# A list schedule that knows the port shared by VectorE and GpSimd, in a one-core decoder layer

## The chip, the core and the metric

The kernel runs on one core of a Trainium2 chip. A core has five engines that run side by side: TensorE (PE, matmuls), VectorE (DVE), ScalarE (ACT), GpSimd (POOL) and SyncE (SP, which only issues transfers here). The metric is the device time of one execution, in microseconds (us).

## What is computed

The reference is one layer of a decoder, 1024 tokens by 1024 features, float32. Cut to what matters:

```python
shift1, scale1, gate1, shift2, scale2, gate2 = silu(c) @ w_ada + b_ada
h = rms_norm(x, norm1) * (1 + scale1) + shift1
q, kc_raw, vc_raw, ks, vs, kw, vw, g, cgate, bgate, u = split(h @ w_in)
# 8 heads, 2 key/value heads; three branches per row of queries
o_c = softmax(q @ compress(kc_raw) + bias) @ compress(vc_raw)
o_s = softmax(q @ ks + bias, causal) @ vs         # blocks of 64; all 16 blocks are selected
o_w = softmax(q @ kw + bias, window 512) @ vw
attn = g[0] * o_c + g[1] * o_s + g[2] * o_w
conv = bgate * conv1d(cgate * u)                  # depthwise, 3 taps
x = x + gate1 * (concat(attn, conv) @ w_out)
h2 = rms_norm(x, norm2) * (1 + scale2) + shift2
out = x + gate2 * (square(relu(h2 @ w_ff1)) @ w_ff2)
```

## The kernel before

Everything is kept feature by feature: a tile has 128 features as partitions and 512 tokens (one half of the sequence) as columns. Every float32 matmul is made of three: an operand is split into a rounded part `hi` (a CAST, by `copy`) and a rest `lo` (a subtraction, by `sub`), and `mm3` adds hi x hi, hi x lo and lo x hi in one PSUM bank. So each 128x512 tile that TensorE reads costs one cast and one subtraction first, weights too.

The stages are, in the order of the program: the opening (adaLN's first part, the norm, and the first three column tiles of the projection); keys, values, queries and the compressed keys; attention of the first half of the tokens, with the convolution's matmuls beside it; attention of the second half, beside which the output projection of the first half and 30 tiles of the MLP's hidden layer are worked out; output projection and second norm of the second half; and the MLP. In the opening, `ada` loads a piece of `w_ada` and VectorE makes a product with a sum over 1024 columns (FA<-FA 128x1024, line 339), from which come one column of `mod` and one of `a`; then each tile k of x is multiplied with the norm (x*y, FA<-FA,FA), scaled by ScalarE, and split. In attention, the sum of a score and its bias is made on VectorE from PSUM (line 358), `nm`, `den` and `cf` are small tiles of three columns per row of queries, the row is scaled by `cf` (line 351 on GpSimd), transposed in blocks of 32 on VectorE (line 365), shuffled by sixteen transfers (FA<-FA, by SP) and split for the product with the values.

No order is written by hand. `Plan` takes down every instruction with a cost in ns and the engines that may run it (`alts`); `issue` makes eight list schedules (`_forward`, each with priorities from a schedule made from the end by `_backward`), keeps the one with the shortest span, and issues each engine's queue in that order. Many casts, subtractions, products and scalings may go to one of two engines (`EW` is VectorE or GpSimd); the schedule gives such an instruction to whichever engine is free first. On the chip each queue then runs strictly in order, and engines wait for each other by semaphores where data demands it. `issue` is called twice: once for everything up to the second norm, and once for the MLP. Memory is a few big tiles cut by hand: FA (FA1, FA2) is float32, RA holds the split operands, `sc`, `fa`, `po`, `stb` and (in the MLP) `pd` are PSUM banks.

Lines that the text speaks of: 293 is every matmul, 311 and 317 are ScalarE's activations and copies, 319 and 321 casts on VectorE and GpSimd, 328 and 330 two-input additions, subtractions and products on VectorE and GpSimd, 339 VectorE's scalar_tensor_tensor, 347 and 351 tensor_scalar on VectorE and GpSimd, 377 every transfer.

Of the kernel before, what the change touches and what calls it, by code (L numbers as in the profile page):

```python
# [37 lines left out]
# ---------------------------------------------------------------- the order of the instructions  # L38
class Op:
    __slots__ = ("alts", "idx", "preds", "succs", "nbytes", "past", "end", "group")  # L40
# [6 lines left out]
class Plan:  # L47
    """Takes down instructions in program order, then issues them in the order of a list schedule.

    An instruction may be taken by any of the engines listed for it.  What depends on what follows  # L50
    from the memory that the instructions read and write.  The first schedule goes by the longest way
    to the end; the next ones by where a schedule made from the end puts the instructions.
    """

    PASSES = 8
    # from the end of an instruction to the start of one that needs it, by their engines
# [5 lines left out]
    def __init__(self, tc):  # L62
        self.tc, self.nc = tc, tc.nc
        self.eng = {"PE": self.nc.tensor, "ACT": self.nc.scalar, "DVE": self.nc.vector,
                    "POOL": self.nc.gpsimd, "SP": self.nc.sync}
        self.ops, self.mem, self.scratch = [], {}, set()
        self.group, self.ahead = "", {}  # how much earlier than its turn a group of instructions goes
        self.free = {e: 0.0 for e in self.eng}  # when the engines are through with what was issued before

    # -- recording  # L70
    @staticmethod
    def _mask(ap):
        """{group of partitions: (first column, last column + 1, columns as bits)}"""
        dims = [tuple(d) for d in ap.ap]
        off = ap.offset
        if ap.space == PSUM:  # one accumulation group at a time in a bank
            return {0: (0, 1, 1)}
# [38 lines left out]
    def op(self, alts, outs, ins, nbytes=0):  # L116
        o = Op(alts, len(self.ops), nbytes)
        o.group = self.group
        for aps, wr in ((ins, False), (outs, True)):
            for ap in aps:  # L120
# [7 lines left out]
                for po, pm, pw in log:  # L128
                    if (wr or pw) and po is not o and self._hit(m, pm):
                        if po.end is None:  # L130
                            o.preds.add(po)
                        else:  # issued before
# [7 lines left out]
    # -- the schedule  # L140
# [3 lines left out]
    def _longest(self):  # L144
        """The longest way from each instruction to the end."""
# [7 lines left out]
    def _forward(self, prio):  # L153
        """[(start, instruction, choice, end)]: whenever an engine is free, the first by priority of those that are ready."""
# [5 lines left out]
        done, order, hw, dma, last, cold = bytearray(len(ops)), [], 0.0, 0.0, self.free["PE"], 0.0  # L160
# [15 lines left out]
        while len(order) < len(ops):  # L176
# [14 lines left out]
            _, idx, i = heapq.heappop(heaps[e])  # L191
            o, cost = ops[idx], ops[idx].alts[i][1]
            done[idx] = 1
            if not o.nbytes:
                if e == "PE":  # at half its rate after a rest
# [5 lines left out]
            else:  # L201
# [7 lines left out]
                if e == "SP":  # what is moved next is left open until its turn is near  # L209
# [10 lines left out]
    def _backward(self, order):  # L220
        """From the end, the last first: how long before the end each instruction starts."""
# [54 lines left out]
    # -- the instructions  # L276
# [11 lines left out]
    def mm(self, out, a, b, start, stop):  # L288
        n, m = self._n(out), self._n(a)
        c = max(0.4167 * n + 2, 107.0)  # L290
# [22 lines left out]
    def copy(self, out, a, engs=("ACT",)):  # L313
# [8 lines left out]
        self.op(alts, [out], [a])  # L322

    def tt(self, out, a, b, op, engs=("DVE",)):
# [6 lines left out]
        self.op(alts, [out], [a, b])  # L331
# [4 lines left out]
    def stt(self, out, a, s, b, op0, op1, accum=None):  # L336
# [3 lines left out]
                [out] + ([accum] if accum is not None else []), [a, b] + ([s] if ptr else []))  # L340

    def ts(self, out, a, s1, s2, op0, op1=None, engs=("DVE",)):
        n, ps, alts = self._n(out), self._ps(a, out), []
        ptr = sum(hasattr(s, "tensor") for s in (s1, s2))
        for e in engs:
# [6 lines left out]
            else:  # a product with one number for each partition  # L352
                alts.append((e, 0.833 * n + 93 + 93 * ptr, lambda: self.nc.scalar.activation(out, a, AF.Copy, scale=s1)))
        self.op(alts, [out], [a] + [s for s in (s1, s2) if hasattr(s, "tensor")])
# [25 lines left out]
class Rot:  # L380
    """A fixed set of tiles, taken in turn."""
# [9 lines left out]
class Region:  # L391
    """A stretch of columns of a tile, handed out from its left end."""
# [20 lines left out]
# columns (of 4 bytes) of the two tiles that everything of the first part lies in  # L413
# [961 lines left out]
```

## Time and profile before

| | |
|---|---|
| time, median of three runs | 1439.66 us (1437.44 to 1443.62) |
| span of the profiled execution, first to last instruction | 1439.1 us |
| instructions | 17186 |
| TensorE busy, mean granted clock | 1293.1 us, 0.955 |
| VectorE busy | 827.2 us |
| ScalarE busy | 608.0 us |
| GpSimd busy | 584.7 us |
| moved by DMA | 220.66 MB, mean 153 GB/s |

The profiled execution's own time is not given apart from its span, which is 0.6 us below the median. An instruction's time in the profile runs from its start on the engine to its end; what it waits for by semaphore comes before the start and is listed as idle time. A wait that the engine takes after the start is part of the duration.

### The profile page before, as it was taken

The page shows a single profiled execution, that of the slowest core. Times are in us where ns is not written, and L with a number is a line of the kernel's source. Part 1 is how long each engine was busy: PE and PEld are TensorE (multiplying, and loading weights), DVE is VectorE, ACT ScalarE, POOL GpSimd, SP SyncE. Part 2 cuts the span into 40 slices and gives each one's busy share as a digit, 9 for nine tenths or more (in the row PEclk, how much of TensorE's full clock was granted, in tenths as well). Part 3 has the DMA queues.
Part 4 walks back from the last instruction along what each step waited for, and adds up shares of the span by engine and source line. Part 5 has one row for each costly group of instructions (what it writes and reads, how often), then busy time and mean ns, then how long its engine had stood idle before and what let it go on. Part 6 is the DMA issues. An engine that isn't in the chain of part 4 may idle for free.

```text
span 1439.1 us, 17186 instructions
## 1 busy us (share of the span) xinstructions
PE 1293.1 (90%) x5608; PEld 1032.0 (72%) x5608; DVE 827.2 (57%) x1697; ACT 608.0 (42%) x1191; POOL 584.7 (41%) x581
## 2 busy tenths in 40 slices
PE   6689899899889888888797897989999999999998
PEld 3468688677667656666675684868888878888886
DVE  5987878789757675668784747541441252133212
ACT  5566647666536465646664434420130022103100
POOL 4733636587637574536574514111221221222120
PEclk8999999999999999989999897989999999999999
DMA  8567976887676864777769613441430232123131
GB/s 290 159 165 211 248 228 214 205 212 199 191 207 194 244 154 151 195 187 190 215 154 251 218 59 123 138 135 30 128 107 30 77 118 70 59 73 103 30 117 59
DMA packets 110029, 220.66 MB, mean 153 GB/s; under 512 B 14841, under 2 KB 40994, under 8 KB 109428
## 3 DMA queue, kind: packets, MB, share of 16 engines
q1 hardware_dynamic: 106196, 204.76, 49.5%
q0 software_dynamic: 3744, 14.81, 3.6%
q8 instruction: 44, 0.72, 0.2%
q14 instruction: 45, 0.37, 0.1%
HBM read 151.77 MB, written 36.80 MB: 131 GB/s over the span
## 4 chain that ended last, share of the span: by engine, by line
PE 49%; DVE 19%; DMA 13%; SPq 7%; issue 5%; POOL 4%; ACT 3%; DVEq 0%; POOLq 0%; ACTq 0%
PE pd L293 35%; SPq L377 7%; PE sc L293 7%; DMA FA<-FA 5%; PE fa L293 5%; DVE RA L328 5%; DVE FA L339 4%; DVE FA L365 3%; DVE FA L328 2%; POOL RA L330 2%; DMA FA<-in_w_ff 2%; DVE FA L358 2%; ACT FA L311 1%; DMA FA<-in_xT 1%; DMA FA<-in_w_ada 1%
## 5 line engine op out<-in xcount | busy, mean ns | idle before, releaser
L330 POOL TENSOR_TENSOR RA<-FA,RA 128x512 fp32r<-128x512 f32 (+4 forms) x193 | 336.5, 1752 | 521.1 <-ACT RA L317 228.2
L317 ACT CAST RA<-FA 128x512 fp32r<-128x512 f32 (+4 forms) x327 | 233.7, 736 | 587.0 <-PE pd L293 279.9
L293 PE MATMUL fa<-RA 128*128 128x512 f32 (+1 forms) x1384 | 411.6, 406 | 23.0 <-ACT FA L311 11.0
L293 PE MATMUL sc<-RA 128*128 128x512 f32 (+6 forms) x1328 | 338.1, 373 | 40.1 <-DVE mx L358 11.7
L293 PE MATMUL pd<-hid,RA 128*128 128x512 f32 x1344 | 339.5, 392 | 0.0
L293 PEld LDWEIGHTS fa<-RA 128*128 128x128 f32 (+1 forms) x1384 | 265.4, 196 | 86.7 <-ACT FA L311 14.0
L328 DVE TENSOR_TENSOR RA<-FA,RA 128x512 fp32r<-128x512 f32 (+4 forms) x214 | 215.5, 1018 | 193.2 <-PE pd L293 90.0
L293 PEld LDWEIGHTS sc<-RA 128*128 128x128 f32 x1328 | 239.5, 196 | 97.4 <-DVE mx L358 16.7
L293 PEld LDWEIGHTS pd<-hid,RA 128*128 128x128 f32 x1344 | 255.0, 190 | 53.4
L293 PE MATMUL pd<-RA 128*128 128x512 f32 x1008 | 267.9, 397 | 12.8 <-DVE RA L319 6.0
L293 PEld LDWEIGHTS pd<-RA 128*128 128x128 f32 x1008 | 191.0, 191 | 59.0 <-DVE RA L328 8.4
L339 DVE SCALAR_TENSOR_TENSOR FA<-pd,mod,FA 128x512 f32<-128x512 f32 x64 | 45.3, 746 | 219.2 <-PE pd L293 219.2
L311 ACT ACTIVATE FA<-FA,nm 128x640 f32<-128x640 f32 (+7 forms) x192 | 114.4, 597 | 42.9 <-DVE nm L347 22.0
L365 DVE STREAM_TRANSPOSE FA<-FA 128x64 f32<-128x64 f32 (+7 forms) x224 | 99.5, 482 | 41.2 <-DMA FA<-FA 23.0
L311 ACT ACTIVATE FA<-FA 128x512 f32<-128x512 f32 (+2 forms) x147 | 87.7, 616 | 25.2 <-DVE FA L339 14.6
L293 PE MATMUL stb<-RA 128*128 128x512 f32 (+1 forms) x192 | 68.5, 401 | 32.3 <-ACT RA L317 18.7
L351 POOL TENSOR_SCALAR FA<-FA,cf 128x64 f32<-128x64 f32 (+8 forms) x121 | 83.4, 701 | 21.7 <-DVE cf L328 18.3
L358 DVE CUSTOM_DVE_ANT_0 FA<-sc,FA 128x64 f32<-128x64 f32 (+5 forms) x192 | 79.9, 449 | 10.5 <-PE sc L293 10.1
L293 PE MATMUL po<-RA 128*128 128x512 f32 (+4 forms) x164 | 51.3, 380 | 21.7 <-ACT RA L317 15.9
L293 PEld LDWEIGHTS stb<-RA 128*128 128x128 f32 x192 | 36.9, 199 | 46.6 <-ACT RA L317 20.0
L321 POOL TENSOR_SCALAR RA<-FA 128x512 fp32r<-128x512 f32 x42 | 31.4, 748 | 88.2 <-DMA FA<-in_w_ff 42.8
L319 DVE CAST hid<-FA 128x512 fp32r<-128x512 f32 x56 | 42.0, 752 | 36.3 <-PE pd L293 18.8
(129 smaller groups left out, 897.6 us busy)
## 6 DMA issues: line engine op xcount, KB each, us to landing
FA<-in_w_ff SPq DMA_DIRECT2D x64, 512.0 KB, 3.6
FA<-FA SPq DMA_DIRECT2D x128, 176.0 KB, 4.0
FA<-in_w_ada SPq DMA_DIRECT2D x64, 256.0 KB, 3.9
FA<-in_w_ff SPq DMA_DIRECT2D x60, 256.0 KB, 3.8
FA<-FA SPq DMA_DIRECT2D x64, 208.0 KB, 5.2
FA<-in_w_cols SPq DMA_DIRECT2D x34, 256.0 KB, 2.9
FA<-in_xT SPq DMA_DIRECT2D x32, 256.0 KB, 4.8
FA<-in_w_ada SPq DMA_DIRECT2D x16, 512.0 KB, 3.6
```

The costliest lines, as they stand in the source:

```text
L293: self.op([("PE", c, lambda: self.nc.tensor.matmul(out, a, b, start=start, stop=stop))], [out], [a, b])
L311: self.op([("ACT", c, lambda: self.nc.scalar.activation(out, a, func, **kw))], outs, ins)
L317: alts.append((e, 0.833 * n + (53 if ps else 93), lambda: self.nc.scalar.copy(out, a)))
L319: alts.append((e, (1.04 if ps else 0.52) * n + 68, lambda: self.nc.vector.tensor_copy(out, a)))
L321: alts.append((e, 0.833 * n + 174, lambda: self.nc.gpsimd.tensor_scalar(out, a, 1.0, 0.0, ALU.mult, ALU.add)))
L328: alts.append((e, 1.04 * n + 68, lambda: self.nc.vector.tensor_tensor(out, a, b, op)))
L330: alts.append((e, 2.11 * n + 148, lambda: self.nc.gpsimd.tensor_tensor(out, a, b, op)))
L339: self.op([("DVE", 1.04 * self._n(out) + 68 + 61 * ptr, lambda: self.nc.vector.scalar_tensor_tensor(out, a, s, b, op0, op1, **kw))], [out] ...
L351: alts.append((e, 0.833 * n + 174 + 83 * ptr, lambda: self.nc.gpsimd.tensor_scalar(out, a, s1, s2, op0, op1)))
L358: self.op([("DVE", 1.04 * self._n(out) + 75, lambda: self.nc.vector.tensor_tensor_reduce(out, a, b, 1.0, init, ALU.add, ALU.max, accum))], ...
L365: self.op([("DVE", 1.04 * self._n(out) + 68, lambda: self.nc.vector.transpose(out, a))], [out], [a])
L377: self.op([(q, c, lambda: e.dma_start(out=out, in_=a))], [out], [a], nbytes=n)
```

## The change

The schedule gets one more resource, `port`: the time until which the port that VectorE and GpSimd share is taken. Each recorded instruction names the engines on which it would use the port: with no operand in PSUM, copies, two-input instructions and tensor_scalar on either engine, and scalar_tensor_tensor on VectorE; with an operand in PSUM only the GpSimd form is named. When VectorE or GpSimd is free while the port is taken, `_forward` passes over the ready instructions that would need it and takes the first other one; if there is none, the engine waits for the port or for the next instruction to become ready. An instruction that uses the port takes it for its planned cost. A tie between the two goes to VectorE, which stands first in the list of engines. The second edit is the planned cost of a matmul of n columns: 0.4375n + 3 and at least 58 ns, where it was 0.4167n + 2 and at least 107. No instruction of the computation is added or removed, and the lists of engines stay the same.

```diff
-    def op(self, alts, outs, ins, nbytes=0):
+    def op(self, alts, outs, ins, nbytes=0, port=()):
         o = Op(alts, len(self.ops), nbytes)
+        o.port = port
...
-            _, idx, i = heapq.heappop(heaps[e])
+            if e in ("DVE", "POOL") and port > t:
+                h, held = heaps[e], []
+                while h and e in ops[h[0][1]].port:
+                    held.append(heapq.heappop(h))
+                    while h and done[h[0][1]]:
+                        heapq.heappop(h)
+                first = heapq.heappop(h) if h else None
+                for x in held:
+                    heapq.heappush(h, x)
+                if first is None:
+                    free[e] = min(port, pend[e][0][0]) if pend[e] and pend[e][0][0] > t else port
+                    continue
+                _, idx, i = first
+            else:
+                _, idx, i = heapq.heappop(heaps[e])
             o, cost = ops[idx], ops[idx].alts[i][1]
+            if e in o.port:
+                port = t + cost
...
-        c = max(0.4167 * n + 2, 107.0)
+        c = max(0.4375 * n + 3, 58.0)
...
-        self.op(alts, [out], [a])
+        self.op(alts, [out], [a], port=("POOL",) if ps else ("DVE", "POOL"))
...
-        self.op(alts, [out], [a, b])
+        self.op(alts, [out], [a, b], port=("POOL",) if self._ps(a, b) else ("DVE", "POOL"))
```

Every queue gets another order. Three places follow; the lines of the changed kernel are numbered 17 higher than those of before.

The first place is the opening, on GpSimd. Its queue before, from its first product x*y (FA_194<-FA_194,FA_198) on; RA<-FA_198 of 384 columns are the weights' subtractions and RA<-FA_194 those of h:

```order
L330 TENSOR_TENSOR FA_194<-FA_194,FA_198 128x512 x3
L330 TENSOR_TENSOR RA<-FA_198,RA 128x384
L330 TENSOR_TENSOR FA_194<-FA_194,FA_198 128x512
L330 TENSOR_TENSOR RA<-FA_198,RA 128x384
L330 TENSOR_TENSOR RA<-FA_194,RA 128x512
L330 TENSOR_TENSOR RA<-FA_198,RA 128x384
L330 TENSOR_TENSOR FA_194<-FA_194,FA_198 128x512 x4
```

and the same queue after the change:

```order
L386 MEMSET FA_194 128x57 x2
L386 MEMSET FA_194 128x2
L347 TENSOR_TENSOR FA_194<-FA_194,FA_198 128x512
L386 MEMSET FA_194 128x57 x2
L347 TENSOR_TENSOR RA<-FA_198,RA 128x2x256
L347 TENSOR_TENSOR RA<-FA_198,RA 128x252 x2
```

Before, the pattern goes on to 13 products, 6 subtractions of 384 columns and 7 of h, 26 in all; after, one product is left and the rows of two blocks of 256 already belong to the next stage. On VectorE, the queue of the opening after the change begins so (FA_198,mod is the product sum of `ada`):

```order
L356 SCALAR_TENSOR_TENSOR FA_198,mod<-FA_198 128x1024 x3
L356 SCALAR_TENSOR_TENSOR FA_194<-stb,FA_194 128x512
L356 SCALAR_TENSOR_TENSOR FA_198,mod<-FA_198 128x1024
L356 SCALAR_TENSOR_TENSOR FA_198<-FA_194,FA_198 128x512
L345 TENSOR_TENSOR FA_194<-FA_194,FA_198 128x512
L356 SCALAR_TENSOR_TENSOR FA_198,mod<-FA_198 128x1024 x2
L345 TENSOR_TENSOR RA<-FA_198,RA 128x384
L345 TENSOR_TENSOR FA_194<-FA_194,FA_198 128x512 x2
L356 SCALAR_TENSOR_TENSOR FA_198,mod<-FA_198 128x1024 x2
L356 SCALAR_TENSOR_TENSOR FA_194<-po,FA_194 128x512
L356 SCALAR_TENSOR_TENSOR FA_198,mod<-FA_198 128x1024 x2
```

Ten of the sixteen product sums stand in these rows, an eleventh comes before the first subtraction of h; before the change, the sums alternated with `a`, `mod` and the subtractions of h from the fourth one on.

The second place is VectorE in the attention of the first half, just before the scores of the fourth group of rows (ISA FA_194,mx is line 358's sum of score and bias, from PSUM). Before:

```order
L328 TENSOR_TENSOR RA<-FA_194,RA 128x512
L328 TENSOR_TENSOR FA_194<-fa_206,FA_194 128x512
L339 SCALAR_TENSOR_TENSOR FA_194<-FA_194,cvw 128x512 x4
L328 TENSOR_TENSOR RA<-FA_194,RA 128x512 x2
L328 TENSOR_TENSOR FA_194<-fa_207,FA_194 128x512
L328 TENSOR_TENSOR RA<-FA_198,RA 128x512
L328 TENSOR_TENSOR RA<-FA_198,RA 128x4x64
L328 TENSOR_TENSOR RA<-FA_198,RA 128x512 x2
```

After:

```order
L356 SCALAR_TENSOR_TENSOR FA_198<-FA_198,sl 128x512
L345 TENSOR_TENSOR cf_189<-cf_189,gates 128x3
L345 TENSOR_TENSOR RA<-FA_198,RA 128x4x64
L345 TENSOR_TENSOR FA_198<-FA_198 128x512
L382 STREAM_TRANSPOSE FA_198<-FA_194 128x4x4x32
L382 STREAM_TRANSPOSE FA_198<-FA_194 128x3x4x32
L382 STREAM_TRANSPOSE FA_198<-FA_194 128x4x32
L345 TENSOR_TENSOR mod<-sc_205,bad 128x4
```

The run of subtractions and convolution steps is broken up: transposes and reads of PSUM, which don't name the port, stand between them.

The third place is VectorE in the second norm of the second half, where TensorE waits for h2 (FA_198<-FA_194,FA_198 is the product x*y, CAST and RA<-FA_198 its split). Before:

```order
L339 SCALAR_TENSOR_TENSOR FA_198<-stb,FA_198 128x512
L339 SCALAR_TENSOR_TENSOR FA_198<-FA_198 128x512
L328 TENSOR_TENSOR FA_198<-FA_194,FA_198 128x512 x3
L319 CAST RA<-FA_198 128x512
L328 TENSOR_TENSOR FA_198<-FA_194,FA_198 128x512
L319 CAST RA<-FA_198 128x512 x2
L328 TENSOR_TENSOR RA<-FA_198,RA 128x512
L328 TENSOR_TENSOR FA_198<-FA_194,FA_198 128x512 x2
```

After:

```order
L345 TENSOR_TENSOR FA_198<-FA_194,FA_198 128x512 x3
L336 CAST RA<-FA_198 128x512
L345 TENSOR_TENSOR FA_198<-FA_194,FA_198 128x512
L336 CAST RA<-FA_198 128x512
L345 TENSOR_TENSOR RA<-FA_198,RA 128x512
L345 TENSOR_TENSOR FA_198<-FA_194,FA_198 128x512
L345 TENSOR_TENSOR RA<-FA_198,RA 128x512
L345 TENSOR_TENSOR FA_198<-FA_194,FA_198 128x512 x3
```

All eight products and all eight subtractions stand on VectorE now; before, two products and five subtractions were GpSimd's.

## Rows read from the trace of the kernel before

**Rows 1.** The page's first part: busy us, share, instructions.

```profile
PE 1293.1 (90%) x5608; PEld 1032.0 (72%) x5608; DVE 827.2 (57%) x1697; ACT 608.0 (42%) x1191; POOL 584.7 (41%) x581
```

**Rows 2.** Busy us by stretch: length, engines (instructions), clock, DMA share, GB/s.

```profile
18.00:84.00 66.00, 44.12 (x154) 29.63 (x152) 62.99 (x85) 33.56 (x59) 49.51 (x33) 0.90 0.56 183
84.00:430.00 346.00, 309.20 (x1473) 250.55 (x1472) 270.96 (x712) 206.89 (x515) 188.75 (x258) 0.96 0.76 211
430.00:820.00 390.00, 328.84 (x1382) 258.47 (x1381) 276.10 (x617) 223.19 (x422) 221.78 (x221) 0.92 0.72 197
820.00:885.00 65.00, 55.52 (x222) 42.65 (x221) 36.17 (x44) 25.09 (x38) 19.68 (x14) 0.89 0.23 75
965.00:1415.00 450.00, 447.55 (x1965) 368.37 (x1963) 127.77 (x164) 81.20 (x103) 88.78 (x38) 1.00 0.25 76
144.00:180.00 36.00, 29.57 (x121) 22.13 (x120) 29.48 (x46) 22.23 (x45) 23.12 (x19) 0.95 0.93 247
```

**Rows 3.** Chain of waits, shares by line, 84 to 430, then 430 to 820.

```profile
by line: PE sc L293 15.4%; PE fa L293 9.7%; DMA FA<-FA 9.4%; issue 7.7%; SPq L377 7.3%; DVE FA L365 4.1%; DVE RA L328 3.9%; DVE FA L339 3.5%; DMA d_k<-FA 3.4%; DVE FA L328 3.2%; DVE FA L358 2.5%; DMA FA<-in_w_vg 2.2%; PE stb L293 2.0%; POOL
by line: SPq L377 19.7%; DMA FA<-FA 11.2%; PE fa L293 9.2%; DVE RA L328 9.0%; issue 8.6%; DVE FA L365 7.2%; DMA FA<-in_w_ff 6.3%; POOL RA L330 5.2%; DVE FA L358 3.9%; ACT FA L311 2.4%; ACT RA L317 1.8%; PE sc L293 1.7%; DVE cf L328 1.2%; DV
```

**Rows 4.** VectorE's groups, 17 to 77.2: count, busy us, mean ns, idle before.

```profile
L339 DVE SCALAR_TENSOR_TENSOR FA<-FA 128x1024 f32<-128x1024 f32 x16 | 26.3, 1654 | 0.0
L328 DVE TENSOR_TENSOR RA<-FA,RA 128x512 fp32r<-128x512 f32 x10 | 9.8, 978 | 0.2 <-ACT RA L317 0.2
L339 DVE SCALAR_TENSOR_TENSOR a<-mod,n,c 128x1 f32<-128x1 f32 x8 | 7.3, 914 | 0.0
L328 DVE TENSOR_TENSOR mod<-mod,bad 128x1 f32<-128x1 f32 x8 | 5.6, 706 | 0.0
```

**Rows 5.** VectorE's lines 339, 328 there: shortest/median/longest ns.

```profile
L339 DVE SCALAR_TENSOR_TENSOR FA<-FA x16: 1208/1222/2307, 19.1 to 69.9; 128x1024 f32<-128x1024 f32 x16
...
L339 DVE SCALAR_TENSOR_TENSOR a<-mod,n,c x8: 207/1084/1316, 26.0 to 73.9; 128x1 f32<-128x1 f32 x8
...
L328 DVE TENSOR_TENSOR mod<-mod,bad x8: 146/776/1230, 23.7 to 72.2; 128x1 f32<-128x1 f32 x8
```

**Rows 6.** Order of time, GpSimd, then VectorE: start us, length us, instruction.

```profile
43.10 2.71 POOL L330 TENSOR_TENSOR RA<-FA,RA 128x512 fp32r<-128x512 f32 x2 [1.53 <-ACT RA L317]
...
43.19 1.76 DVE L328 TENSOR_TENSOR RA<-FA,RA 128x512 fp32r<-128x512 f32 x1
...
61.07 0.68 DVE L328 TENSOR_TENSOR RA<-FA,RA 128x512 fp32r<-128x512 f32 x1
```

**Rows 7.** GpSimd's groups, 17 to 77.2.

```profile
L330 POOL TENSOR_TENSOR FA<-FA,FA 128x512 f32<-128x512 f32 x13 | 23.8, 1849 | 18.0 <-DVE FA L339 18.0
```

**Rows 8.** TensorE's groups, 23 to 84.2.

```profile
L293 PE MATMUL sc<-RA 128*128 128x512 f32 x96 | 34.4, 437 | 21.0 <-DVE RA L328 10.6 <-DVE RA L319 8.2 <-POOL RA L330 1.5
```

**Rows 9.** Order of time, TensorE: the opening's first and last matmul.

```profile
29.56 0.79 PE L293 MATMUL sc<-RA 128*128 128x512 f32 x1 [6.55 <-DVE RA L319]
...
83.91 0.39 PE L293 MATMUL fa<-RA 128*128 128x512 f32 x1
```

**Rows 10.** VectorE's groups, 84 to 820.

```profile
L328 DVE TENSOR_TENSOR RA<-FA,RA 128x512 fp32r<-128x512 f32 x114 | 106.7, 946 | 59.9 <-ACT RA L317 30.5 <-POOL RA L321 8.7 <-PE po L293 7.2
...
L328 DVE TENSOR_TENSOR cf<-cf,gates 128x3 f32<-128x3 f32 x37 | 16.7, 461 | 0.6
```

**Rows 11.** VectorE's `cf`, whole span: shortest/median/longest ns.

```profile
L328 DVE TENSOR_TENSOR cf<-cf,gates x37: 111/163/3423, 248.7 to 746.8; 128x3 f32<-128x3 f32 x37
```

**Rows 12.** Order of time, VectorE, second norm.

```profile
868.29 4.04 DVE L328 TENSOR_TENSOR FA<-FA,FA 128x512 f32<-128x512 f32 x3
872.25 0.41 DVE L319 CAST RA<-FA 128x512 fp32r<-128x512 f32 x1
...
886.18 0.69 DVE L328 TENSOR_TENSOR RA<-FA,RA 128x512 fp32r<-128x512 f32 x1
```

**Rows 13.** Order of time, TensorE, second norm.

```profile
874.73 4.35 PE L293 MATMUL pd<-RA 128*128 128x512 f32 x7 [5.97 <-DVE RA L319]
```

More of the change, by code (lines that the diff above doesn't have):

```diff
@@ L39 @@
 class Op:
-    __slots__ = ("alts", "idx", "preds", "succs", "nbytes", "past", "end", "group")
+    __slots__ = ("alts", "idx", "preds", "succs", "nbytes", "past", "end", "group", "port")
     def __init__(self, alts, idx, nbytes):
@@ L159, in _forward @@
         heaps, pend = ({e: [] for e in self.eng} for _ in range(2))
-        done, order, hw, dma, last, cold = bytearray(len(ops)), [], 0.0, 0.0, self.free["PE"], 0.0
+        done, order, hw, dma, last, cold, port = bytearray(len(ops)), [], 0.0, 0.0, self.free["PE"], 0.0, 0.0
         def push(o):
@@ L339, in stt @@
         self.op([("DVE", 1.04 * self._n(out) + 68 + 61 * ptr, lambda: self.nc.vector.scalar_tensor_tensor(out, a, s, b, op0, op1, **kw))],
-                [out] + ([accum] if accum is not None else []), [a, b] + ([s] if ptr else []))
+                [out] + ([accum] if accum is not None else []), [a, b] + ([s] if ptr else []), port=() if self._ps(a, b) else ("DVE",))
     def ts(self, out, a, s1, s2, op0, op1=None, engs=("DVE",)):
@@ L353, in ts @@
                 alts.append((e, 0.833 * n + 93 + 93 * ptr, lambda: self.nc.scalar.activation(out, a, AF.Copy, scale=s1)))
-        self.op(alts, [out], [a] + [s for s in (s1, s2) if hasattr(s, "tensor")])
+        self.op(alts, [out], [a] + [s for s in (s1, s2) if hasattr(s, "tensor")], port=("POOL",) if ps else ("DVE", "POOL"))
     def ttr(self, out, a, b, init, accum):
```

## The prediction

> **What bounds the kernel now.** TensorE is busy for 90% of the span [rows 1], so I first asked where the other 10% and its slow-clock time lie, with the busy times by stretch. From 965 to 1415 us TensorE is busy 447.55 of 450 us at a granted clock of 1.00, with 1965 matmuls, 0.229 us each; there another order of the vector work can bring nothing [rows 2]. Before that it is short everywhere: 44.12 of 66 us at a clock of 0.90 in the opening (18 to 84), 309.20 of 346 in the projections and the first half's attention, 328.84 of 390 at 0.92 in the second half's attention, and 55.52 of 65 around the second norm [rows 2]. That is 22, 37, 61 and 9 us of idle, 129 in all; this is the pool that the change can draw on, with what the lower clock costs on top.
>
> Then the chain of waits, to see who is late there. Between 84 and 820 us it is broken: shuffle transfers (FA<-FA), the SP queue's own time (7.3% and 19.7%), TensorE, and VectorE in many small pieces [rows 3]. No engine is the bound; each piece of VectorE or GpSimd work on the chain is latency.
>
> Last I looked at how long equal instructions take, since that is what the change is about. In the opening VectorE works almost without a pause from 17.7 to 77.1 us. A one-column `mod` add takes 146 ns at the least and 706 on average; a one-column `a` takes 207 and 914; the 1024-column product sum takes 1208 and 1654 [rows 4, 5]. The order of time shows why: GpSimd starts a pair of subtractions at 43.10, and VectorE's next one, started at 43.19, takes 1.76 us, while the same instruction at 61.07, with GpSimd idle, takes 0.68 [rows 6]. So VectorE stands still behind GpSimd's instruction, and everything queued on it stands too. GpSimd pays as well: its x*y products in the opening average 1849 ns, against 1.36 us for each of that pair [rows 6, 7].
>
> **The change part by part.** *The edit to the scheduler's matmul cost* (0.4167n + 2, at least 107, to 0.4375n + 3, at least 58) turns 215 ns into 227 for 512 columns; the trace has 229 [rows 2]. It makes the plan's TensorE a little slower and truer; I cost it at nothing of its own. *The port* does two things. It moves work: the built program has 130 fewer instructions on GpSimd, 82 more on VectorE and 48 more on ScalarE. And it reorders: while one of the two holds the port, the other is given work that doesn't need it.
>
> *Opening.* GpSimd's 26 additions and subtractions become 1; 12 products x*y, 6 subtractions of 384 columns and 7 of 512 go to VectorE, 2 casts leave it. The time that VectorE stood blocked, from counts and means against the shortest: product sums 16 x (1654 - 1208) = 7.1, `a` 8 x (914 - 207) = 5.7, `mod` 8 x (706 - 146) = 4.5, subtractions 10 x (978 - 680) = 3.0; with 4 us for the smaller groups (an estimate, a fifth of these 20.3) 24 us of the 59.4 [rows 4 to 6]. Without it 35 remain. The moved work adds 19 x 0.68 and, by columns from that, 6 x 0.54; the two casts take off 0.8: 35 + 12.9 + 3.2 - 0.8 = 50 us, so VectorE's run ends 9 us earlier. TensorE has 144 matmuls there (96 on the sc banks and 48 on fa), 33 us at 0.229, and took from 29.56 to 84.3, 21.0 us of it idle [rows 8, 9]. After the change ten of VectorE's sixteen product sums stand in its first eleven rows, some 21 us of work with all that comes before the first h subtraction, so TensorE starts in earnest near 39 us and can then run almost without a break: 39 + 33, and 3 for the lower clock (a tenth of 33, as now), give 75 against 84.3. I take -9. Bounds: -13 if it starts some 4 us sooner, on the parts of h that ScalarE makes; 0 if the loads of w_ada come late. The DMA share is 0.56 here, so I lean to the gain [rows 2].
>
> The Trainium skill ("Perfetto Trace Analysis", Optimizing Scalar/DVE Operations) warns that moving operations between VectorE and GpSimd might not help, since the two share a port. By that rule this term would be 0 and the sum 1427. The trace speaks against it: an x*y product costs 1849 ns on GpSimd and an addition of that size 680 on VectorE when nothing stands in the way [rows 6, 7].
>
> *Middle, 84 to 820 us.* Blocked on VectorE: subtractions of 512 columns 114 x (946 - 680) = 30 of 106.7 us, `cf` 37 x (461 - 163) = 11 of 16.7 [rows 6, 10, 11], a third of both. VectorE's port instructions (RA L328, FA L339, FA L328, cf L328) make 10.6% of the chain before 430 and 10.2% after it, 37 + 40 us [rows 3]; if a third of that is blocked, 25 us could go. GpSimd's 5.2% after 430 (20 us) could give 5 more at the same rate as VectorE's, less for its longer instructions [rows 3]. Ceiling -30. Two things cut it. The order on chip follows the plan only as far as the plan's clock is right, for VectorE and GpSimd are tied together by data alone. And the next chain, shuffles and SP, is close. I take about a quarter of the ceiling: -8, and 0 as the floor of a gain. The work that moves here is about 40 additions, 22 us on VectorE at 0.55 (an estimate between the sizes above). It takes the place of slower ones on GpSimd, and VectorE has gaps to take it (547 + 22 of 736 us, 77% [rows 2]), so I cost it at nothing; without those gaps it costs the 22.
>
> *Second norm, 868 to 887.* TensorE waits here for every piece (5.97 us in front of one group of matmuls) [rows 13]. VectorE's run goes from 868.29 to 886.87, 18.6 us, three products at its head taking 4.04 where 0.68 each would do [rows 6, 12]. GpSimd has no part in this stretch afterwards, and VectorE's run is 8 products and 8 subtractions at 0.68, 4 casts at 0.41 and one subtraction of 1024 columns at 1.2: 13.7 us. That is -5; I take -4, for ScalarE's casts. In the MLP behind it VectorE takes some 18 more subtractions while TensorE is full: nothing.
>
> Sum: 1439.1 (the span) - 9 - 8 - 4 = 1418; the runs' median is 0.6 us above the span, which I leave out.
>
> **The rivals.** *The plan's order doesn't hold on chip.* The queues are in order, and where a transfer is late the plan's instants shift by microseconds, so that in the middle an instruction meets the other engine's as often as before. For it: transfers are much of the chain there [rows 3]. Against: fewer GpSimd instructions alone make fewer meetings. Middle 0: 1426. The Trainium skill ("SBUF — State Buffer", Who interferes with whom) says that issue order decides who blocks, which is the ground for this rival; the pair at 43.10 and 43.19 agrees [rows 6]. *The opening's gain is given back at the transfers.* From 144 to 180 us the DMA share is 0.93 [rows 2]; if that load sets the pace and doesn't shift with its producers, the 9 us are lost there: 1427. Against it: those transfers carry what the engines made. *VectorE becomes the bound in the middle.* It is busy 78% and 71% there now [rows 2] and gets 22 us more. If the blocked time falls by less than that, the middle grows, and the sign turns when the middle loses more than the 13 us that the opening and the norm bring. At its full price, all 22 on the chain: 1439 - 13 + 22 = 1448. *The change does nothing that counts*: the next chain takes up both the opening and the middle: 1435.
>
> **How the numbers follow.** A time can be told from no change at about 0.5% (7 us). Chances: the forecast, 1405 to 1425, 0.50; the first rival 0.12, the second 0.10, both mostly on the fast side; VectorE as the bound 0.13; nothing that counts 0.10; a middle near its ceiling, 1396, 0.05. Faster is the forecast, the deep middle and most of the first two rivals, 0.71; same 0.16; slower 0.13. The range leaves out the slow rival and some of the deep end: 1394 to 1441.
>
> **What would show it.** Right: in the opening, one-column `mod` and `a` near their shortest, and the last first-stage matmul near 75 us; `cf` on VectorE well below 461 ns in the middle; the second norm's run at about 14 us; VectorE's busy time no higher than now in spite of 82 more instructions. Wrong: TensorE idle between 84 and 820 no less than 98 us, VectorE over 77% busy there, or VectorE waiting for w_ada in the opening.

## The result, and the profile after

The changed kernel takes 1395.2 us (median of four runs, 1392.65 to 1401.58), the kernel before 1439.88 beside it (four runs, 1437.44 to 1443.62). The ratio is 0.9696 [0.9667, 0.9726]: 44.7 us less, where the prediction had 22. The sign was right; the time lies in the range, at its low end, but below the 1405 to 1425 us of the forecast itself. The profiled execution of the changed kernel is one of 1397.07 us with a span of 1395.3.

The first part of its page answers to [rows 1]:

```profile
PE 1278.4 (92%) x5608; PEld 1030.4 (74%) x5608; DVE 756.4 (54%) x1779; ACT 632.7 (45%) x1239; POOL 384.1 (28%) x451
```

VectorE has 82 instructions more and is busy 71 us less; GpSimd has 130 fewer and 201 us less. TensorE runs the same 5608 matmuls in 14.7 us less, and its idle time (span less busy) falls from 146.0 to 116.9: 29.1 and 14.7 make the 44 us of the span.

Where they came from is read best between events that both kernels have, and not at equal instants, since everything in the changed kernel lies earlier. I took from TensorE's order of time the end of the opening's last matmul, the first matmul on a pd bank (the second norm), the 24th (the MLP in full swing) and the last. Busy time between these, before (length, engines, clock, DMA share, GB/s, as in [rows 2]):

```profile
84.30:434.00 349.70, 312.06 (x1480) 252.84 (x1480) 274.37 (x720) 208.18 (x517) 191.89 (x261) 0.96 0.76 211
84.30:874.70 790.40, 686.49 (x3061) 548.09 (x3060) 572.63 (x1359) 450.54 (x968) 424.04 (x488) 0.94 0.71 195
874.70:889.50 14.80, 11.08 (x23) 6.94 (x24) 12.07 (x15) 4.44 (x6) 6.17 (x4) 0.52 0.30 98
889.50:965.00 75.50, 69.52 (x295) 56.31 (x294) 43.26 (x51) 26.47 (x36) 14.87 (x7) 0.95 0.47 147
965.00:1435.30 470.30, 467.81 (x2053) 384.80 (x2051) 131.89 (x169) 81.20 (x103) 88.78 (x38) 1.00 0.25 75
```

and after:

```profile
73.50:422.00 348.50, 317.55 (x1501) 259.74 (x1501) 264.95 (x757) 224.74 (x557) 148.12 (x234) 0.95 0.77 213
73.50:843.20 769.70, 679.32 (x3060) 548.85 (x3059) 527.18 (x1391) 470.55 (x1009) 317.52 (x407) 0.94 0.73 201
843.20:854.80 11.60, 9.05 (x24) 6.50 (x25) 11.60 (x21) 8.19 (x12) 0.00 (x0) 0.59 0.27 87
854.80:921.00 66.20, 63.25 (x275) 51.51 (x274) 34.93 (x53) 25.62 (x35) 0.00 (x0) 0.97 0.50 159
921.00:1391.40 470.40, 470.40 (x2073) 386.25 (x2071) 125.23 (x188) 81.04 (x104) 61.89 (x26) 1.00 0.24 77
```

The opening ends 10.8 us earlier (84.3 to 73.5), the middle is 20.7 shorter (790.4 to 769.7), the second norm (to the 24th matmul) 3.2, and the MLP, the last two rows, 9.2 (545.8 to 536.6, for 2348 matmuls in both). That is 43.9. The middle's gain is made of 13.5 us less idle on TensorE (103.9 to 90.4) and 7.2 less busy; the MLP's, in the same way, of 5.5 less idle (8.5 to 3.0) and 3.7 less busy. The first rows of the two fences go to the last d_attn transfer of the first half (434 and 422): that part takes as long as before, but 21 more matmuls are done in it.

The opening, VectorE's groups from 12 to 73.5 us, against [rows 4]:

```profile
L356 DVE SCALAR_TENSOR_TENSOR FA<-FA 128x1024 f32<-128x1024 f32 x16 | 20.2, 1283 | 3.8 <-ACT FA L334 2.7 <-DMA FA<-in_w_ada 1.1
L345 DVE TENSOR_TENSOR RA<-FA,RA 128x512 fp32r<-128x512 f32 x20 | 12.9, 679 | 2.6 <-PE fa L310 1.9 <-ACT RA L334 0.7
L356 DVE SCALAR_TENSOR_TENSOR a<-mod,n,c 128x1 f32<-128x1 f32 x8 | 1.6, 206 | 0.0
L345 DVE TENSOR_TENSOR mod<-mod,bad 128x1 f32<-128x1 f32 x8 | 1.2, 146 | 0.0
```

`mod` falls from a mean of 706 to 146 ns, `a` from 914 to 206, the subtractions from 978 to 679: the means now stand at what were the shortest before [rows 5, 6]. The loads of w_ada cost 1.1 us. TensorE's order of time, against [rows 9]:

```profile
37.77 0.79 PE L310 MATMUL sc<-RA 128*128 128x512 f32 x1 [9.93 <-ACT RA L334]
...
73.10 0.39 PE L310 MATMUL fa<-RA 128*128 128x512 f32 x1
```

It starts 8 us later and then runs its 144 matmuls almost without a gap.

VectorE's groups from 84 to 820 us, against [rows 10]:

```profile
L345 DVE TENSOR_TENSOR RA<-FA,RA 128x512 fp32r<-128x512 f32 x142 | 105.2, 757 | 44.1 <-ACT RA L334 25.1 <-PE sc L310 7.8 <-PE fa L310 4.5
```

28 more subtractions take 1.5 us less: the mean goes from 946 to 757, where 680 is one that isn't blocked [rows 6]. The stretch as a whole, against the second and third of [rows 2]:

```profile
84.00:820.00 736.00, 649.50 (x2935) 526.43 (x2934) 506.32 (x1355) 451.50 (x975) 309.34 (x401) 0.94 0.75 206
```

TensorE is idle for 86.5 us of it (98 before), VectorE busy for 506 (547 before). The chain of waits from 430 to 820, against the second of [rows 3]:

```profile
by line: PE fa L310 18.4%; SPq L394 14.6%; PE sc L310 11.5%; DMA FA<-FA 6.8%; DMA FA<-in_w_ff 6.2%; issue 5.4%; PE stb L310 5.4%; POOL RA L347 4.7%; DMA d_x<-FA 3.9%; ACT FA L328 2.8%; DMA FA<-d_tab 2.3%; DVE FA L382 2.3%; DMA FA<-in_xT 2.1
```

VectorE's subtractions (RA), 9.0% before, are no longer among the entries shown, of which the smallest has 2.1%; the share of the matmuls on fa is twice the old one; and SP's queue (19.7 to 14.6%) and the shuffles (11.2 to 6.8%) fell too. (From 84 to 430 SP's share rose from 7.3 to 9.3%.) In the second norm VectorE's order of time, against [rows 12], is

```profile
840.92 1.89 DVE L345 TENSOR_TENSOR FA<-FA,FA 128x512 f32<-128x512 f32 x3
...
853.71 1.28 DVE L345 TENSOR_TENSOR RA<-FA,RA 128x512 fp32r<-128x512 f32 x2
```

a run of 14.1 us in place of 18.6.

In the MLP the prediction put the gain at nothing. The kernel before there, GpSimd and then VectorE in order of time:

```profile
956.00 5.18 POOL L330 TENSOR_TENSOR RA<-FA,RA 128x1024 fp32r<-128x1024 f32 x2 [23.40 <-PE pd L293]
...
957.01 1.95 DVE L328 TENSOR_TENSOR FA<-FA 128x512 f32<-128x512 f32 x1
958.99 2.75 DVE L339 SCALAR_TENSOR_TENSOR FA<-FA,sl 128x512 f32<-128x512 f32 x1
961.66 0.74 DVE L339 SCALAR_TENSOR_TENSOR FA<-pd,mod,FA 128x512 f32<-128x512 f32 x1
962.32 0.67 DVE L328 TENSOR_TENSOR FA<-FA 128x512 f32<-128x512 f32 x1
```

The addition that takes 0.67 us alone takes 1.95 behind GpSimd's pair. The chain of waits of the kernel before goes through just these:

```profile
946.48 9.18 PE pd L293 x29
957.01 1.96 DVE FA L328
958.99 2.81 DVE FA L339 x2
963.05 63.32 PE pd L293 x275
...
1027.81 1.71 DVE hid L319
...
1031.42 126.46 PE pd L293 x556
```

and after the change it is one piece from 909.68 to the end:

```profile
909.68 481.75 PE pd L310 x2118
```

### The profile page after: what moved, and what is told of

Its sections match the earlier page's. It is cut to its first block, busy times and chain, and to the rows that moved or that the text cites. A ratio compares the mean times of both kernels' runs of the same rounds, so it can differ in the third digit from the quotient of the medians.

```text
span 1395.3 us, 17129 instructions
## 1 busy us (share of the span) xinstructions
PE 1278.4 (92%) x5608; PEld 1030.4 (74%) x5608; DVE 756.4 (54%) x1779; ACT 632.7 (45%) x1239; POOL 384.1 (28%) x451
## 4 chain that ended last, share of the span: by engine, by line
PE 60%; DMA 16%; DVE 9%; SPq 7%; ACT 3%; issue 3%; POOL 2%; DVEq 0%; ACTq 0%; POOLq 0%
PE pd L310 37%; PE sc L310 10%; PE fa L310 10%; SPq L394 7%; DMA FA<-FA 4%; DMA FA<-in_w_ada 2%; PE stb L310 2%; DVE FA L356 2%; DVE RA L345 2%; DMA FA<-in_w_ff 2%; ACT FA L328 1%; DVE FA L382 1%; POOL RA L347 1%; DVE FA L345 1%; DVE FA L375 1%
## 5 line engine op out<-in xcount | busy, mean ns | idle before, releaser
L334 ACT CAST RA<-FA 128x512 fp32r<-128x512 f32 (+5 forms) x343 | 243.0, 731 | 593.1 <-PE pd L310 275.8
L310 PE MATMUL fa<-RA 128*128 128x512 f32 (+1 forms) x1384 | 398.5, 405 | 27.9 <-ACT RA L334 8.4
L347 POOL TENSOR_TENSOR RA<-FA,RA 128x512 fp32r<-128x512 f32 (+2 forms) x131 | 218.2, 1679 | 604.1 <-PE pd L310 375.6
L310 PE MATMUL sc<-RA 128*128 128x512 f32 (+6 forms) x1328 | 326.6, 371 | 30.1 <-ACT RA L334 13.6
L345 DVE TENSOR_TENSOR RA<-FA,RA 128x512 fp32r<-128x512 f32 (+4 forms) x276 | 223.3, 836 | 182.8 <-PE pd L310 105.3
L382 DVE STREAM_TRANSPOSE FA<-FA 128x64 f32<-128x64 f32 (+8 forms) x224 | 97.5, 481 | 68.1 <-DMA FA<-FA 56.4
L328 ACT ACTIVATE FA<-FA,nm 128x64 f32<-128x64 f32 (+6 forms) x192 | 114.3, 597 | 25.3 <-POOL nm L368 18.9
L368 POOL TENSOR_SCALAR FA<-FA,cf 128x64 f32<-128x64 f32 (+7 forms) x90 | 61.8, 694 | 29.9 <-DVE cf L345 22.7
L338 POOL TENSOR_SCALAR RA<-FA 128x512 fp32r<-128x512 f32 x35 | 23.7, 678 | 145.6 <-PE sc L310 51.6
L370 ACT ACTIVATE FA<-FA,cf 128x64 f32<-128x64 f32 (+8 forms) x102 | 58.6, 615 | 9.9 <-DVE cf L345 6.7
```

The lines of the kernel that those rows point to most:

```text
L310: self.op([("PE", c, lambda: self.nc.tensor.matmul(out, a, b, start=start, stop=stop))], [out], [a, b])
L328: self.op([("ACT", c, lambda: self.nc.scalar.activation(out, a, func, **kw))], outs, ins)
L334: alts.append((e, 0.833 * n + (53 if ps else 93), lambda: self.nc.scalar.copy(out, a)))
L338: alts.append((e, 0.833 * n + 174, lambda: self.nc.gpsimd.tensor_scalar(out, a, 1.0, 0.0, ALU.mult, ALU.add)))
L345: alts.append((e, 1.04 * n + 68, lambda: self.nc.vector.tensor_tensor(out, a, b, op)))
L347: alts.append((e, 2.11 * n + 148, lambda: self.nc.gpsimd.tensor_tensor(out, a, b, op)))
```

## The experiments

Four theories stood in the expectations. A: the port in the plan is what counts; A' adds that at least half of it comes from the new order around the port. B: it is only that work leaves GpSimd. C: a large part comes from the truer matmul cost. Later came S (the new matmul cost by itself loses 15 to 22 us) and N (list schedules of this program scatter by 10 to 15 us, whatever the edit). Each ratio is against the kernel before on the same chip (medians 1437.9 to 1442.0).

**One edit at a time.** The kernel before with the new matmul cost alone:

```diff
-        c = max(0.4167 * n + 2, 107.0)
+        c = max(0.4375 * n + 3, 58.0)
```

> The kernel before with the new matmul cost alone, no port. Theory A (the port is what counts): within 0.5% of before, 1433 to 1447 us, with GpSimd still at 578 instructions and the opening's last matmul near 84 us. Theory C (a truer TensorE in the plan is a large part of the gain, above all in the MLP, where I had forecast nothing and 9 us came): 1415 to 1430.

Measured: 1459.94 us, ratio 1.0159 [1.0124, 1.0195], above both ranges. And the changed kernel with the old matmul cost:

```diff
-        c = max(0.4375 * n + 3, 58.0)
+        c = max(0.4167 * n + 2, 107.0)
```

> The changed kernel with the old matmul cost, port kept. Theory A: 1390 to 1402 us, as the change. Theory C: 1408 to 1425.

Measured: 1379.23 us, ratio 0.9590 [0.9562, 0.9618], below both ranges. C falls: the truer cost alone makes the kernel slower, and the port alone makes it faster than the whole change.

**Who runs it, or when.** The change lets the plan choose both. `issue` was made to plan twice; the first plan fixes the engine of every instruction, the second sets the order:

```diff
+        best = self._plan(True)        # with the port
+        for _, o, i, _ in best[1]:
+            o.alts = [o.alts[i]]
+        best = self._plan(False)       # without it
```

This keeps the changed kernel's engines (451 instructions on GpSimd) and orders them as if there were no port.

> Every instruction on the engine that the change's schedule gives it (456 on GpSimd), but then scheduled once more without the port, so that nothing is passed over. Theory B (the work that leaves GpSimd is the gain, since fewer GpSimd instructions are fewer to stand behind): 1393 to 1405 us. Theory A' (the reordering around the port is at least half of it): 1412 to 1430. In both the opening, where GpSimd keeps one addition, ends near 74 us.

Measured: 1403.8 us, ratio 0.9771 [0.9722, 0.9821], in B's range. With True and False exchanged, the engines are those of a plan without the port, and the order knows it:

> Every instruction on the engine that the schedule without the port gives it (579 on GpSimd), then scheduled with the port known. Theory B: 1428 to 1442 us, near before, and VectorE's cf adds above 400 ns. Theory A': 1405 to 1420, with cf below 300 ns. The opening ends later than 80 us in both.

Measured: 1457.33 us, ratio 1.0130 [1.0098, 1.0161], above both ranges; `cf` takes 419 ns, as B had it. Both have the new matmul cost, so they stand against the first experiment's 1459.94. The engines alone bring 56 us of the 65 that lie between that and the changed kernel; the order alone brings 3. Each of these is a single plan, and plans scatter by up to 20 us (below): the 3 is not to be told from nothing, the 56 is. Against the means of the plans without and with the port at this cost (1453.7 and 1384.0, below) the engines alone bring 50 us of 70. A' falls as it was put, by which half or more should come from the order; whether the order is worth the rest once the engines are right isn't shown. By stage, from TensorE's order of time (us):

| kernel | opening ends | middle | second norm | MLP |
|---|---|---|---|---|
| before | 84.3 | 790.4 | 14.8 | 545.8 |
| changed | 73.5 | 769.7 | 11.6 | 536.6 |
| new matmul cost alone | 85.0 | 806.4 | 15.5 | 547.6 |
| port alone | 72.1 | 756.1 | 13.5 | 530.9 |
| engines alone | 74.8 | 779.8 | 11.1 | 532.9 |
| order alone | 93.6 | 803.4 | 12.1 | 544.4 |
| GpSimd dear (below) | 82.0 | 784.5 | 14.7 | 544.6 |
| nothing on GpSimd (below) | 75.7 | 765.8 | 14.4 | 532.7 |

Against the new matmul cost alone, the engines bring 10, 27, 4 and 15 us; the order brings 3 in three of the stages each and loses 9 in the opening.

The time that VectorE stands blocked doesn't tell the two apart. Its subtractions from 84 to 820 us, 970 ns on average with the new matmul cost alone, with the engines alone and then with the order alone:

```profile
L354 DVE TENSOR_TENSOR RA<-FA,RA 128x512 fp32r<-128x512 f32 x138 | 108.3, 795 | 38.3 <-ACT RA L343 18.8 <-PE fa L319 4.3 <-PE po L319 4.0
L354 DVE TENSOR_TENSOR RA<-FA,RA 128x512 fp32r<-128x512 f32 x105 | 82.3, 795 | 32.7 <-ACT RA L343 23.1 <-DMA FA<-in_w_out 2.3 <-POOL RA L347 1.9
```

Both bring the mean down to 795 ns, but the middle is 27 us shorter with the one and 3 with the other. So a shorter subtraction isn't by itself a shorter middle.

**How many, or which.** Then B: the kernel before, without the port, with GpSimd's two-input instructions at double cost, so that as few are left there (448 against 451). The number is not all that this moves: the plan's clock for GpSimd is wrong by the same factor, and no run held the two apart.

```diff
-                alts.append((e, 2.11 * n + 148, lambda: self.nc.gpsimd.tensor_tensor(out, a, b, op)))
+                alts.append((e, 4.22 * n + 296, lambda: self.nc.gpsimd.tensor_tensor(out, a, b, op)))
```

> The kernel before with one number changed: GpSimd's two-input instruction is planned at twice its cost (4.22n + 296). No port, the old matmul cost. It leaves 453 instructions on GpSimd, as the change does. Theory B (work off GpSimd is the gain, and the port in the plan is one way to get it): 1375 to 1400 us. Theory A' (the plan must know the port): 1415 to 1440.

Measured: 1437.62 us, ratio 0.9980 [0.9961, 0.9999]. So B falls as a matter of number. VectorE's subtractions, and its casts of the hidden layer, whole span, here:

```profile
L328 DVE TENSOR_TENSOR RA<-FA,RA 128x512 fp32r<-128x512 f32 x170 | 139.9, 831 | 58.3 <-ACT RA L317 45.2 <-PE fa L293 4.0 <-POOL RA L321 4.0
L319 DVE CAST hid<-FA 128x512 fp32r<-128x512 f32 x56 | 44.2, 793 | 38.7 <-PE pd L293 18.8 <-ACT FA L311 12.6 <-DMA FA<-d_hid 7.2
```

and with the engines alone:

```profile
L354 DVE TENSOR_TENSOR RA<-FA,RA 128x512 fp32r<-128x512 f32 x182 | 137.5, 769 | 55.0 <-ACT RA L343 20.8 <-PE sc L319 11.6 <-PE fa L319 8.1
L345 DVE CAST hid<-FA 128x512 fp32r<-128x512 f32 x56 | 24.2, 448 | 26.9 <-DMA FA<-d_hid 11.5 <-PE pd L319 10.6 <-ACT FA L337 4.6
```

With the same number on GpSimd, one cast takes 793 ns in the first and 448 in the second. In the opening a dearer GpSimd keeps other work than the port leaves: seven products x*y, at 1864 ns each, and ten subtractions, where the port leaves one product. Behind it the kinds of work are nearly the same: in the middle GpSimd has 81 subtractions of 512 columns and 31 casts here, 75 and 35 with the engines alone; in the MLP 27 subtractions of 1024 columns and 9 other instructions here, 26 and none there. What differs behind the opening is thus which single instructions these are, and when they meet VectorE's; how much either counts isn't shown. The other end, the port with the old matmul cost and GpSimd struck out wherever another engine may run the instruction (80 stay):

```diff
+        alts = [a for a in alts if a[0] != "POOL"] or alts
```

> Port and old matmul cost as in the port-only kernel (1379), but GpSimd is struck from every list that has another engine; it keeps 85 instructions. Theory B taken to its end (every instruction off GpSimd is a gain): 1360 to 1378 us. Against it (VectorE and ScalarE become the bound in the first 800 us, where GpSimd still does useful work beside PSUM reads and transposes): 1385 to 1430.

Measured: 1392.6 us, ratio 0.9670 [0.9631, 0.9709], not in B's range but in the other. VectorE's subtractions from 84 to 820:

```profile
L346 DVE TENSOR_TENSOR RA<-FA,RA 128x512 fp32r<-128x512 f32 x217 | 145.0, 682 | 40.6 <-ACT RA L335 28.0 <-PE sc L311 8.0 <-issue 2.3
```

682 ns is the unblocked length: nothing is in the way, and VectorE carries 217 of them. What GpSimd still does in the port's plan is worth 13 us against 1379.23, which the scatter below can hide, and nothing against 1395.2. The Trainium skill ("Perfetto Trace Analysis", Optimizing GPSIMD Operations) advises other engines where possible; here that gives as much as the change does (47 us and 45), though at the old matmul cost.

**The MLP by itself.** The port known only to the second call of `issue`, old matmul cost:

```diff
+        self.use_port = self.free["PE"] > 0
```

> The port in the second schedule alone (the MLP), old matmul cost. If the 9 us that the change won behind the second norm are the MLP's own (subtractions of weights and of the hidden layer off GpSimd, fewer stops between its parts): 1428 to 1434 us, and the MLP from its 24th matmul to the end at 537 or less against 546. If they came with the first schedule (its tail hands buffers and transfers over sooner): 1437 to 1441.

Measured: 1428.57 us, ratio 0.9929 [0.9901, 0.9956]. From the 24th pd matmul to the end it takes 532.3 us (545.8 before). Its chain of waits there has TensorE in one piece:

```profile
942.45 478.14 PE pd L312 x2115
```

So the MLP is a term of its own, 11 us.

**The matmul cost again, and scatter.** The changed kernel lies 16 us above the port alone; is that the new matmul cost? Its slope alone, with the port and the old floor (0.4375n + 3, at least 107):

> The changed kernel with the matmul's new slope (0.4375n + 3) and the old floor of 107 ns. If the slope is what costs the 16 to 22 us that the new matmul cost was seen to cost: 1391 to 1400 us. If the floor is (64 to 128 columns planned at 58 ns, sooner done in the plan than on the chip): 1376 to 1384. A value far from both would say that any small change of the plan moves the time by that much.

Measured: 1394.51 us, ratio 0.9682 [0.9656, 0.9708], in the range for the slope, which spoke for S. But then the old cost was moved by a quarter of a per cent, half a nanosecond per matmul, either way, which has no meaning by itself:

```diff
-        c = max(0.4167 * n + 2, 107.0)
+        c = max(0.4157 * n + 2, 107.0)
```

> The port-only kernel with the matmul's slope nudged down by a quarter of a per cent (0.4157n + 2, floor 107), half a nanosecond for 512 columns. Nothing in the plan is truer or falser by it. Theory S (a truer TensorE in the plan is what costs 15 to 22 us): 1376 to 1382 us, as the port-only kernel. Theory N (list schedules scatter; any new plan lies within some 15 us of another): a value at least 5 us from 1379, and one or both nudges nearer to 1390.

Measured: 1391.54 us, ratio 0.9672 [0.9639, 0.9706], outside S's range and as N had it. The other way, 0.4177:

> The same, nudged up by as much (0.4177n + 2). Theory S: 1376 to 1382 us. Theory N: at least 5 us from 1379 here or in the other nudge.

Measured: 1373.25 us, ratio 0.9549 [0.9492, 0.9606], outside S's range again. The kernel before with 0.4177:

> The kernel before, without a port, nudged up by as much (0.4177n + 2). Theory S: 1435 to 1445 us. Theory N: the same scatter as with the port, 1425 to 1460; then the 22 us of the new matmul cost without the port are scatter too, and the port's own gain is known only to that.

Measured: 1438.83 us, ratio 0.9992 [0.9969, 1.0016], inside both ranges. And the port with a slope that is much too low, 0.39:

> The port-only kernel with TensorE planned 7% too fast (0.39n + 2, floor 107: 202 ns where the chip takes 227). Theory S, a plan that errs towards a fast TensorE is better: 1370 to 1379 us. Theory N: anywhere from 1375 to 1400, without a trend.

Measured: 1378.07 us, ratio 0.9582 [0.9551, 0.9613], inside both ranges again. The same nudge was then given to the new cost (0.4365 and 0.4385 for 0.4375), with the port:

> The changed kernel (port, new matmul cost) with the slope nudged down (0.4365n + 3, floor 58). If the new slope is itself the loss of 15 us: 1388 to 1402 us, as the change, here and in the nudge up. If the change's 1395 is one draw of a scatter of some 10 us around 1381: 1370 to 1390 in at least one of the two.

> The same, nudged up (0.4385n + 3): 1388 to 1402 us if the slope is the loss, 1370 to 1390 here or there if it is scatter.

Measured: 1381.8 us, ratio 0.9578 [0.9541, 0.9614], and 1375.1 us, ratio 0.9538 [0.9499, 0.9578]; and without it:

> The kernel before, without a port, new matmul cost nudged down (0.4365n + 3, floor 58). If the new slope is the loss: 1452 to 1468 us, as the matmul-only kernel (1460). If scatter: 1430 to 1450 in at least one of the two.

> The same, nudged up (0.4385n + 3): 1452 to 1468 us if the slope is the loss, 1430 to 1450 here or there if scatter.

Measured: 1448.42 us, ratio 1.0064 [1.0042, 1.0086], and 1452.72 us, ratio 1.0088 [1.0058, 1.0119]: the first lies in the range for scatter, the second in that for a loss. Together (us):

| matmul cost | without the port | with the port |
|---|---|---|
| old, and nudged | 1439.9, 1438.8 | 1379.2, 1391.5, 1373.3 |
| new, and nudged | 1459.9, 1448.4, 1452.7 | 1395.2, 1381.8, 1375.1 |

With the port the two rows have means of 1381.3 and 1384.0: S falls there, and N holds, with more scatter than it said (18 and 20 us in a row). Without the port the plans of a row lie closer (1 and 12 us apart), and the new cost is 9 to 21 us slower in all three. The port itself is worth 58 us at the old cost (1439.3 to 1381.3) and 70 at the new (1453.7 to 1384.0). The change as given has the slowest of the three plans at its cost; the two nudged upwards, 1373.25 and 1375.1 us, beat both kernels.

Most of the scatter lies in the middle. In the eight kernels that know the port throughout and may still use GpSimd (the changed one, the port alone, and the six with other slopes or floors), the middle takes 749.9 to 772.9 us, 760 on average, against 784.1 to 807.5 in the five without it; the opening ends between 71.6 and 74.9 us against 84.3 to 88.4, and the MLP takes 530.1 to 538.1 us against 545.7 to 547.6. So each of the three is shorter in every plan with the port than in any without it. The changed kernel has the second longest middle of its eight.

## Why the prediction was half right

**Opening, -9: right, by its own steps.** It came out at -10.8. TensorE started at 37.77 (39 was said) and ended at 73.49 (75); VectorE's one-column groups fell to their shortest. The term is the surest of all: in all eight plans with the port the last matmul ends between 71.6 and 74.9 us, with the engines alone at 74.8, and at 93.6 with the order alone.

**Middle, -8: the term that was mis-sized.** It measured -20.7, and -34 with the port alone. The step that failed is "I take about a quarter of the ceiling", and with it both reasons for the cut: over the eight plans with the port the middle is 17.5 to 40.5 us shorter than before, 30 on average, which is the ceiling itself. The first was that the order on chip follows the plan only as far as the plan's clock is right. True or not, it bears on the order, and the order alone brought the middle 3 us; the engines brought 27, and an instruction stays with its engine whatever the chip's clock does. The second was that the next chain, shuffles and SP, is close. It wasn't a fixed chain: after 430 SP's share and the shuffles' fell with VectorE's, and only before it SP's rose. The ceiling of 30 itself was too low for the port alone, because it counted only what VectorE and GpSimd held of the chain: 7.2 us of the changed kernel's 20.7 are the same matmuls in less busy time on TensorE, and 12.3 of the port alone's 34 (686.49 to 674.21). The granted clock is a part of that at most: in the middle TensorE is busy at half clock (0.50) for 69.6 us before, 65.3 in the changed kernel and 56.2 with the port alone, so that some 2 and 7 us are its due (an estimate: half of what fell away, as the same matmul takes 0.79 us at half clock and 0.39 at full [rows 9]). The rest is open.

That the blocked time goes was right for the subtractions: their excess over 680 ns was 114 x 266 = 30 us and is 142 x 77 = 11. It wasn't all of the gain, as the order alone showed. The sign that I had named with it, `cf` well below 461 ns, came true (266) but says nothing: `cf` takes 244 ns in the slowest kernel, the one with the new matmul cost alone, 346 with the port alone and 512 with the engines alone. That the moved work costs nothing was right too: VectorE is busy 41 us less between 84 and 820 with 27 more instructions.

**Second norm, -4: right**, -3.2, with the run at 14.1 (13.7 was said).

**MLP, "while TensorE is full: nothing": wrong**, -9.2 here and -11 by itself. TensorE is full from 965 to 1415 [rows 2], and I carried that to the whole MLP. The stretch just before it, which none of the rows shows and which the pool of 129 us leaves out, isn't full:

```profile
885.00:965.00 80.00, 73.83 (x305) 59.74 (x306) 45.03 (x55) 26.47 (x36) 14.87 (x7) 0.93 0.49 151
```

Even behind 965 TensorE lost 2.5 us (470.30 less 467.81) where casts of `hid` and subtractions stood behind GpSimd. The two steps together make up nearly all of the 22.7 us by which the prediction fell short: 12.7 in the middle and 9.2 here.

**Matmul cost, "at nothing of its own": wrong without the port** (+9 to +21 us), and not to be told from scatter with it. Why a truer cost gives a worse plan there is open; so is whether it is more than chance, with three plans against two.

**The rivals.** VectorE as the bound fell: it runs 82 more instructions in 71 us less. The opening's gain given back fell: the first half's last d_attn transfer is 12 us earlier, and all of the opening's 10.8 is still there. That the plan's order doesn't hold was half a truth: the order by itself brought nothing that can be told from scatter, but most of the gain was not in the order. The Trainium skill ("Perfetto Trace Analysis", Optimizing Scalar/DVE Operations) says that moving operations between VectorE and GpSimd might not help; here the moves are most of the gain, if they are chosen by the port, and bring nothing when they are chosen by a dearer GpSimd.

**What stays open.** Which instructions make the difference between two assignments with equal numbers was seen in the casts and the opening, not tried one by one. Why the engines shorten the middle and the order alone doesn't, with the same mean subtraction, is open too. And why one plan with the port is 20 us faster than its neighbour isn't settled: the middle takes 769.7 us in the changed kernel and 749.9 in the fastest at its cost, from the same rules.

## What to carry to other kernels

Where two engines block each other, first ask which of them should run an instruction, and only then when: freeze the engines and change the order, then the other way round, and the two are told apart with two kernels, or better with a few nudged plans of each. When a term is sized from a chain of waits, read every stretch of the span, the seemingly full one too, and don't cut the sum for a next chain that waits for the same late work. Before a single list schedule's time is laid to an edit of its costs, nudge a cost by a meaningless amount: here that moved the time by up to 20 us, as much as the edit in question.

## What the runs showed of the hardware

An instruction of one column can stand as long as one of 1024: `mod` took up to 1.23 us behind GpSimd [rows 5] and 143 to 149 ns without it, and of three columns `cf` took up to 3.42 us [rows 11]. That one stood through three of GpSimd's instructions in a row, and not only through the one that was running when it started. Before the change, GpSimd and then VectorE in order of time:

```profile
602.87 3.62 POOL L330 TENSOR_TENSOR RA<-FA,RA 128x1024 fp32r<-128x1024 f32 x2
606.47 0.61 POOL L321 TENSOR_SCALAR RA<-FA 128x512 fp32r<-128x512 f32 x1
...
603.66 3.42 DVE L328 TENSOR_TENSOR cf<-cf,gates 128x3 f32<-128x3 f32 x1
```

It starts inside the first of the pair at 602.87 and ends at 607.08, with the last of the three. GpSimd's work beside VectorE was worth little here: taking nearly all of it away, 500 instructions, left the kernel at 1392.6 us, 47 below where it was, though 13 above the port alone.
